# Rotary queries and keys projected as feature rows instead of token rows, and a list scheduler with other landing times

## The chip, the cores and the metric

The kernel runs on one core of one Trainium2 chip. The metric is device time in microseconds of that core. All arithmetic is float32; most large products are made of three passes over operands that were split into a high and a low part (type fp32r).

## What is computed

One layer of a hybrid encoder over 1024 tokens of width 1024: a SwiGLU network, a mixing part, a second SwiGLU network, each with an RMS norm before and behind it. The mixing part is what the change touches:

```python
z = _rmsnorm(h, mix_pre_g[l]) @ w_in[l]
y_att = _attention_group(z[..., :ATT_IN], cos, sin, attn_out_g[l])      # 8 heads of 64
y_rwkv = _rwkv7_group(z[..., ATT_IN:], ...)                             # 8 heads, two directions
mix = jnp.concatenate([y_att, y_rwkv], axis=-1) @ w_out[l]
...
def _rope(t, cos, sin):                      # queries and keys, per head
    half = t.shape[-1] // 2
    t1, t2 = t[..., :half], t[..., half:]
    return jnp.concatenate([t1 * c - t2 * s, t2 * c + t1 * s], axis=-1)
```

The first 1536 columns of `w_in` give queries, keys and values (512 each), the other 1920 feed the RWKV-7 scan. Attention is softmax over three dilated bands; the scan runs forward and backward in blocks.

## The kernel before, in words

The program is written as straight code, but nothing is issued while it runs. Each engine call is noted on a tape (`_Tape.note`); at the end `_Tape.order` chooses an order and `_Tape.play` issues it. So every instruction of the profile stands at one line, that of `play` (L512 before, L565 in the changed kernel), and instructions are told apart by their tiles.

The order comes from a list scheduler. `_Tape.cost` gives each operation a time on its engine (`took`), a time until others may use its result (`late`), and for transfers a time on the wire (`moved`). `_Tape.sweep` walks through time and gives each engine the ready operation of best rank; `_Tape.order` runs it forward and backward a few times, keeps the best order by its own reckoning, then adds the hand-set offsets of the table `LEADS` (from operation, to operation, offset of rank) and sweeps once more. On the chip each engine, and each queue of transfers, takes its own list strictly in turn; waits between engines follow from the data.

The stages in time: first network (to about 690 us of the span), projection of the scan's inputs (`project_rwkv`), projection of queries, keys and values (`project_tokens`), attention (`attention`, with `far` and `near`), the scan (`prep`, `solve`, `merge`, `chain`) interleaved with all of these from the projections on, the output projection (`project_attended`, `finish_unit`, `out_project`) and the second network.

In `project_tokens` a block of 256 columns of `w_in` is loaded (`columns`: tile `zraw`, split into `zh` and `zl`). For each of eight groups of 128 tokens, 24 matmuls of 256 columns make the bank `zq` with tokens as rows. For queries and keys ScalarE copies it to `zz`, VectorE multiplies it by two tables (`rope`, 32 loads) and adds (`zo`), TensorE turns it by two transposes (`zt`, with the identity), ScalarE copies the high part and a plain copy (`zts`), VectorE takes the low part, and GpSimd issues the stores: one to `d_qf` or `d_kf`, and two to `d_kk` for keys or four to `d_q` for queries, in rows of 128 floats. Values need only the copy and one store (`d_va`).

In `project_rwkv` the same kind of product is made the other way round: features are rows, two banks `zr` of 128 by 512 hold all 1024 tokens, and each of 48 matmuls is 512 columns wide.

Other names that the prediction speaks of: `X` (from `d_x`) is what a block's solve works on, by 62 small operations on `ttmp` and `Ti`, on GpSimd for blocks 1 to 5 and on VectorE for the others; its result goes to `d_t` and `d_tt` and comes back as `d` and `tt` for the matmuls `pa` and `pb`. `th_w`, `th_a`, `in` are loads of `prep`, `bk` and `pr` its products, `lp` and `bp` its matmuls, `lm` what is kept of `lp`. `xu`, `st` and `y` are the matmuls of the recurrence itself. `s`, `pt` and `po` (64 columns) are attention's scores, transposes and values. At its end `ya` goes to `d_ya`, comes back as `yat`, is scaled and turned (`yq`) and multiplied by the output weights (`wor`, split into `woh` and `wol`; `po` with 512 columns).

Of the kernel before, what the change touches and what calls it, by code (L numbers as in the profile page):

```python
# [32 lines left out]
def _ap(src, off, pat):  # L33
# [58 lines left out]
class _Op:  # L92
    __slots__ = ("eng", "method", "args", "kwargs", "out", "ins", "after", "preds", "succs", "took", "late", "load", "rank",
                 "left", "ready", "start", "end", "n", "moved", "follow", "taken", "frees", "grid", "cell", "port")


class _Tape:
# [3 lines left out]
    FREE, NEAR = ("ps_w",), 3000  # L101
    GATED = {"s3": 0, "s12": 0, "pt3": 0, "pt12": 0, "lp": 0, "bp": 0, "yq": 0, "gate": 1, "bonus": 1, "op": 2}

    def __init__(self, tc):
        self.tc, self.nc = tc, tc.nc
        self.ops, self.pools, self.home, self.stacks, self.now, self.hold = [], [], {}, {}, 0, []
        for name in self.NAMES:
            setattr(self, name, _Voice(self, name))
        self.masks = {}
        self.base, self.top = -(-tc.nc.sbuf_base // 32) * 32, tc.nc.sbuf_top  # L110
# [52 lines left out]
    def wire(self):  # L163
# [83 lines left out]
        for op in self.nodes:  # L247
            op.preds, op.succs = list(given[op]), []
# [5 lines left out]
    def cost(self, op):  # L254

        op.load = op.moved = 0
# [6 lines left out]
        if op.method == "dma_start":  # L263
# [7 lines left out]
            op.moved = max((9.5 * runs + 0.0366 * size) / 16, size / (3.6 * rows))  # L271
        elif op.eng == "tensor":
# [86 lines left out]
    def sweep(self, back=False):  # L359
# [11 lines left out]
        push, pop = heapq.heappush, heapq.heappop  # L371

# [17 lines left out]
        while True:  # L390
# [54 lines left out]
            if e == "tensor":  # L445
                took = self.pace(last, op, t - free[e])
                last, follow = op, op.follow
                if not back:
                    while t >= edge + 3413:
                        part = busy / 3413  # L450
                        cold, busy, edge = part < 0.56 or cold and part < 0.885, 0.0, edge + 3413
                    took = took * 2 if cold else took
                    busy += took * (0.5, 0.8, 1.0)[op.grid[0] // 64]
# [13 lines left out]
            settle(op, end)  # L467
            if not back:
# [12 lines left out]
    def order(self, rounds=5):  # L481
# [4 lines left out]
        for k in range(rounds):  # L486
            out, span = self.sweep()
            if best is None or span < best[1]:
                best = out, span, {op: (op.start, op.end) for op in out}, {op: op.rank for op in self.nodes}
# [6 lines left out]
        for op, (a, b) in best[2].items():  # L496
            op.start, op.end = a, b
# [9 lines left out]
    def play(self, ops):  # L507
# [3 lines left out]
        for op in ops:  # L511
            i = getattr(getattr(self.nc, op.eng), op.method)(*op.args, **op.kwargs).ins  # L512
# [144 lines left out]
class _Kernel:  # L657
# [264 lines left out]
    def columns(self, p, c0, n, tiles=None, tag="zraw", bufs=4):  # L922

        hl = tiles or [[p.tile([128, n], F32R, name="z" + c, tag="z" + c, bufs=12) for c in "hl"] for k in range(NK)]
# [26 lines left out]
    def project_tokens(self, p, psum, x):  # L951

        nc, V, A, G, T = self.nc, self.nc.vector, self.nc.scalar, self.nc.gpsimd, self.nc.tensor
        for b, g in [(b, g) for b in (1, 0, 2) for g in range(2)]:
            hl = self.columns(p, b * 512 + g * 256, 256)
            for t in range(NT):
                ts = slice(t * 128, t * 128 + 128)
                ps = psum.tile([128, 256], F32, name="zq", tag="w")
                self.token_major(ps, x, t, hl)
                z = p.tile([128, 4, 2, 32], F32, name="zz", tag="zz", bufs=3)  # L960
                A.activation(z.rearrange("p a b c -> p (a b c)"), ps, AF.Copy, scale=-HD ** -0.5 if b == 0 else 1.0)
                if b == 2:
                    G.dma_start(self.v_att[ts, g * 256:g * 256 + 256], z.rearrange("p a b c -> p (a b c)"))
                    continue
                cs = p.tile([128, 2, 2, 32], F32, name="rope", tag="rope", bufs=2)
                self.load(cs.rearrange("p a b c -> p (a b c)"), self.io["k_rope"][ts, :])
                o, y = (p.tile([128, 4, 2, 32], F32, name="z" + n, tag="z" + n, bufs=1) for n in "oy")
                V.tensor_tensor(o, z, cs[:, None, 0].to_broadcast([128, 4, 2, 32]), op=OP.mult)
                V.tensor_tensor(y, z[:, :, ::-1, :], cs[:, None, 1].to_broadcast([128, 4, 2, 32]), op=OP.mult)
                V.tensor_tensor(o, o, y, op=OP.add)  # L970
                q = psum.tile([128, 2, 128], F32, name="zt", tag="o")
                of = o.rearrange("p a b c -> p (a b c)")
                for i in range(2):
                    T.transpose(q[:, i, :], of[:, i * 128:(i + 1) * 128], self.ident)
                y = p.tile([128, 2, 128], F32, name="zts", tag="zts", bufs=2)
                w = p.tile([128, 2, 2, 128], F32R, name="zt", tag="zt", bufs=2)
                h, l = w[:, :, 0], w[:, :, 1]
                A.activation(h, q, AF.Copy)
                V.tensor_tensor(l, q, h, op=OP.subtract)
                A.activation(y, q, AF.Copy)  # L980
                G.dma_start((self.q_d, self.kt_d)[b][g * 2:g * 2 + 2, :, ts].rearrange("a p t -> p a t"), y)
                for d, v in zip(self.qk_d[b], (w, w[:, :, ::-1])):
                    for i in range(2):
                        G.dma_start(_ap(d, (g * 512 + i * 256) * S + t * 128, [[2 * S, 128], [S, 2], [1, 128]]),
                                    v[:, i].bitcast(F32))

    def project_rwkv(self, p, psum, x, blocks):

        nc, V, A, T = self.nc, self.nc.vector, self.nc.scalar, self.nc.tensor
        for c0, n in blocks:  # L990
            hl = self.columns(p, ATT + c0 * 128, n * 128)
            for ct in range(c0, c0 + n):
                cs = slice((ct - c0) * 128, (ct - c0 + 1) * 128)
                ps = [psum.tile([128, 512], F32, name="zr", tag="w") for half in range(2)]
                for k, (h, l) in enumerate(hl):
                    for half in range(2):
                        for i, (w, j) in enumerate(((h, 0), (h, 1), (l, 0))):
                            T.matmul(ps[half], w[:, cs], x[half][j][:, k, :], start=(k == 0 and i == 0),
                                     stop=(k == NK - 1 and i == 2))
# [907 lines left out]
```

## Time and profile before

| | |
|---|---|
| median of 3 runs | 2240.51 us (2238.98 to 2243.06) |
| the profiled execution | 2226.97 us, span 2225.2 us |
| mean granted TensorE clock | 0.985 |
| busy | TensorE 2138.5 us, weight loads 1776.4, VectorE 1551.0, ScalarE 1041.7, GpSimd 724.2 |

All times below are of the profiled execution, counted from the start of its span. A matmul's duration in the rows includes the way through the array, which overlaps the next one: what a matmul costs is the distance from one start to the next. A matmul of plain float32 stands as two records, so 32 records of `lp` are 16 calls. "q" behind an engine's name means its queue of transfers.

### The profile page before, as it was taken

The numbers are of one execution on the slowest core, as the hardware profiler recorded it, in microseconds if no ns is written. First come the engines' busy times: TensorE is split into PE (matmuls) and PEld (weight loads), VectorE is DVE, ScalarE is ACT, GpSimd is POOL, SyncE is SP. The second block draws the span as 40 slices with busy tenths as digits, with TensorE's granted clock in tenths as the row PEclk, the third lists the DMA queues.
The fourth block names the chain that finished last, engine by engine and source line by source line (L and its number), as shares of the span: only waits on it lengthen the run. The fifth ranks groups of instructions, "written<-read, shape, count | busy, mean of one in ns | idle before, by whom it ended". The sixth has DMA issues, their size and how long they took to land.

```text
span 2225.2 us, 41159 instructions
## 1 busy us (share of the span) xinstructions
PE 2138.5 (96%) x15236; PEld 1776.4 (80%) x15236; DVE 1551.0 (70%) x2630; ACT 1041.7 (47%) x2021; POOL 724.2 (33%) x1070
## 2 busy tenths in 40 slices
PE   7999999999999999999889998999899999999998
PEld 5888888888877887999777887777788888878886
DVE  8787778775575665764465567659987878877565
ACT  6333323354466655553556676456533233335453
POOL 2344444520000001569366571312053444441000
PEclk9999999999999999999899999999999999999999
DMA  5354454586563339875887656675454444558665
GB/s 151 127 181 152 154 168 142 185 276 201 174 206 105 131 149 279 229 231 164 232 223 199 180 154 169 168 258 167 123 180 142 169 158 142 171 171 288 195 206 171
DMA packets 370749, 404.52 MB, mean 182 GB/s; under 512 B 76402, under 2 KB 279026, under 8 KB 370548
## 3 DMA queue, kind: packets, MB, share of 16 engines
q1 hardware_dynamic: 320256, 294.79, 44.4%
q0 software_dynamic: 32240, 98.64, 12.4%
q10 hardware_dynamic: 18052, 8.46, 1.4%
q8 instruction: 120, 1.97, 0.4%
q14 instruction: 81, 0.66, 0.1%
HBM read 267.50 MB, written 134.28 MB: 181 GB/s over the span
## 4 chain that ended last, share of the span: by engine, by line
PE 73%; DVE 9%; DMA 6%; POOL 5%; issue 4%; ACT 3%; SPq 1%; ACTq 0%; DVEq 0%; POOLq 0%
PE gu L512 34%; PE pd L512 17%; PE zr L512 5%; PE po L512 3%; DVE row L512 3%; PE pt L512 2%; PE s L512 2%; PE lp L512 2%; POOL d_q L512 2%; PE xu L512 1%; DVE wl L512 1%; PE zq L512 1%; DVE s L512 1%; PE y L512 1%; POOL Ti L512 1%
## 5 line engine op out<-in xcount | busy, mean ns | idle before, releaser
L512 ACT ACTIVATE wh<-raw 128x512 fp32r<-128x512 f32 x264 | 161.5, 627 | 396.6 <-PE gu L512 257.7
L512 DVE TENSOR_TENSOR wl<-raw,wh 128x512 fp32r<-128x512 f32 x264 | 238.8, 917 | 73.7 <-PE gu L512 39.7
L512 DVE TENSOR_TENSOR row<-gu,row 128x512 f32<-128x512 f32 x308 | 203.1, 683 | 88.0 <-PE gu L512 50.7
L512 PE MATMUL gu<-xh,wl 128*128 128x512 f32 x704 | 239.3, 393 | 1.1 <-DVE wl L512 1.1
L512 POOL TENSOR_TENSOR row<-row 128x512 f32<-128x512 f32 x88 | 119.6, 1359 | 362.3 <-DVE row L512 324.0
L512 PE MATMUL gu<-xh,wh 128*128 128x512 f32 x704 | 234.5, 394 | 1.5 <-ACT xh L512 1.4
L512 PE MATMUL gu<-xl,wh 128*128 128x512 f32 x704 | 233.2, 392 | 1.7 <-DVE xl L512 1.7
L512 DVE TENSOR_TENSOR gwl<-graw,gwh 128x512 fp32r<-128x512 f32 (+1 forms) x176 | 114.0, 654 | 101.3 <-PE pd L512 84.1
L512 PE MATMUL pd<-gl,gwh 128*128 128x512 f32 x616 | 182.3, 392 | 0.0
L512 PE MATMUL pd<-gh,gwh 128*128 128x512 f32 x616 | 181.3, 391 | 0.4 <-ACT gh L512 0.4
L512 PE MATMUL pd<-gh,gwl 128*128 128x512 f32 x616 | 180.2, 391 | 0.7 <-DVE gwl L512 0.7
L512 ACT ACTIVATE gwh<-graw 128x512 fp32r<-128x512 f32 (+1 forms) x176 | 100.8, 575 | 146.6 <-PE pd L512 123.5
L512 PEld LDWEIGHTS gu<-xh,wl 128*128 128x128 f32 x704 | 132.8, 189 | 29.4 <-DVE wl L512 1.9
L512 PEld LDWEIGHTS gu<-xh,wh 128*128 128x128 f32 x704 | 132.5, 189 | 29.3 <-ACT xh L512 2.2
L512 PEld LDWEIGHTS gu<-xl,wh 128*128 128x128 f32 x704 | 132.5, 189 | 28.8 <-DVE xl L512 2.0
L512 POOL DMA_DIRECT2D d_hid<-row x154 | 84.8, 552 | 168.9 <-DVE row L512 166.0
L512 PEld LDWEIGHTS pd<-gh,gwl 128*128 128x128 f32 x616 | 116.1, 189 | 25.5 <-DVE gwl L512 1.1
L512 PEld LDWEIGHTS pd<-gl,gwh 128*128 128x128 f32 x616 | 116.0, 189 | 24.7 <-DVE gl L512 0.3
L512 PEld LDWEIGHTS pd<-gh,gwh 128*128 128x128 f32 x616 | 115.3, 188 | 24.8 <-ACT gh L512 0.8
L512 ACT ACTIVATE gh<-raw 128x512 fp32r<-128x512 f32 x160 | 99.5, 629 | 53.3 <-PE pd L512 31.8
L512 DVE TENSOR_TENSOR gl<-raw,gh 128x512 fp32r<-128x512 f32 x160 | 112.1, 711 | 15.3 <-ACT gh L512 15.1
L512 POOL TENSOR_TENSOR ws<-ws 128x512 f32<-128x512 f32 x88 | 121.5, 1381 | 2.8
(296 smaller groups left out, 5141.8 us busy)
## 6 DMA issues: line engine op xcount, KB each, us to landing
d_hid<-row POOLq DMA_DIRECT2D x154, 256.0 KB, 2.5
graw<-d_hid SPq DMA_DIRECT2D x132, 256.0 KB, 2.7
raw<-in_ffn_w_gate_dram SPq DMA_DIRECT2D x88, 256.0 KB, 3.1
raw<-in_ffn_w_up_dram SPq DMA_DIRECT2D x88, 256.0 KB, 3.2
ws<-in_ffn_w_down_dram SPq DMA_DIRECT2D x88, 256.0 KB, 3.7
d_ws<-ws POOLq DMA_DIRECT2D x88, 256.0 KB, 2.8
raw<-d_ws SPq DMA_DIRECT2D x88, 256.0 KB, 3.0
raw<-in_ffn_w_down_dram SPq DMA_DIRECT2D x66, 256.0 KB, 3.5
```

Of the source, the lines that this page charges most:

```text
L512: i = getattr(getattr(self.nc, op.eng), op.method)(*op.args, **op.kwargs).ins
```

## The change

`project_tokens` is left with the values. Queries and keys go to a new function, `project_heads`, ahead of it: `columns` as before, then `features` (the inner part of `project_rwkv`, made a function) gives for each pair of heads two banks with features as rows. The halves of a head lie 32 rows apart, so four copies of 32 rows each on ScalarE, scaled, put the other half's rows beside (`zy`); VectorE multiplies the bank by one table, GpSimd the copy by the other, VectorE adds (`zo`), ScalarE copies the high part and VectorE takes the low one (`zt`). The transposes and the copy `zts` are gone. The table is loaded once, 1 MB with features as rows. The stores are whole rows of 1024 floats on SyncE's queue: two for each pair of keys, three for each pair of queries.

The buffers `zraw` go from 4 to 3, `zh` and `zl` from 12 to 11; a 96-column tile that only took space is dropped.

In the scheduler a transfer's `late` depends on its kind and size and has 900 ns more (`SPARE`), and a load's wire time is stretched (`slow`). `LEADS` has 25 rows in place of 34, for the new numbering. The class `_Spare` and the code around it could put extra matmuls into gaps of TensorE; nothing makes one, so none is issued.

```diff
 LEADS = (
-    (165, 245, -11262), (278, 411, 5699), (301, 311, -2969), (425, 453, -5871), (4022, 4045, -7113),
...
+    (130, 157, 14327), (434, 485, -4800), (1581, 1591, 18529), (4285, 4286, -7275), (4305, 4317, -16401),
...
@@ cost
             op.moved = max((9.5 * runs + 0.0366 * size) / 16, size / (3.6 * rows))
+            if op.eng == "gpsimd":
+                op.late = 2150 - 0.9 * min(op.moved, 1000) + self.SPARE
+            elif x.tensor.name in self.home:
+                op.late, op.slow = 1700 + 0.46 * op.moved + self.SPARE, 1.28
+            else:
+                op.late = 900 + 1.05 * op.moved + self.SPARE
@@ sweep
             if op.moved and not back:
                 wire = max(wire, own) + op.moved
-                end = wire - op.moved
-                lanes[e == "gpsimd"].append(wire + op.late)
+                end = own + (wire - op.moved - own) * op.slow
+                lanes[e == "gpsimd"].append(end + op.moved + op.late)
...
+    def project_heads(self, p, psum, x):
+
+        nc, V, A, G = self.nc, self.nc.vector, self.nc.scalar, self.nc.gpsimd
+        turns = p.tile([128, 2, S], F32, name="rope", tag="rope", bufs=1)
+        self.load(turns, self.io["k_rope"].rearrange("(c p) t -> p c t", p=128))
+        for b, g in [(b, g) for b in (1, 0) for g in range(2)]:
             hl = self.columns(p, b * 512 + g * 256, 256)
...
+            for c in range(2):
+                ps = self.features(psum, x, hl, c)
+                o, y = p.tile([128, S], F32, name="zo", tag="us"), p.tile([128, S], F32, name="zy", tag="u", bufs=1)
+                w = p.tile([128, 2, S], F32R, name="zt", tag="zt", bufs=1)
+                for half in range(2):
+                    sl = slice(half * 512, half * 512 + 512)
+                    for q in range(0, 128, 32):
+                        A.activation(y[q:q + 32, sl], ps[half][q ^ 32:(q ^ 32) + 32], AF.Copy, scale=self.qk_scale[b])
+                    V.scalar_tensor_tensor(o[:, sl], ps[half], self.qk_scale[b], turns[:, 0, sl], op0=OP.mult, op1=OP.mult)
+                    G.tensor_tensor(y[:, sl], y[:, sl], turns[:, 1, sl], op=OP.mult)
+                    V.tensor_tensor(o[:, sl], o[:, sl], y[:, sl], op=OP.add)
+                    A.activation(w[:, 0, sl], o[:, sl], AF.Copy)
+                    V.tensor_tensor(w[:, 1, sl], o[:, sl], w[:, 0, sl], op=OP.subtract)
+                pr = g * 2 + c
+                nc.sync.dma_start((self.q_d, self.kt_d)[b][pr], o)
+                for d, v in zip(self.qk_d[b], (w, w[:, ::-1])):
+                    nc.sync.dma_start(_ap(d, pr * 256 * S, [[2 * S, 128], [S, 2], [1, S]]), v.bitcast(F32))
+
+    def features(self, psum, x, hl, c):
+
+        cs = slice(c * 128, (c + 1) * 128)
+        ps = [psum.tile([128, 512], F32, name="zr", tag="w") for half in range(2)]
+        for k, (h, l) in enumerate(hl):
+            for half in range(2):
+                for i, (w, j) in enumerate(((h, 0), (h, 1), (l, 0))):
+                    self.nc.tensor.matmul(ps[half], w[:, cs], x[half][j][:, k, :], start=(k == 0 and i == 0),
+                                          stop=(k == NK - 1 and i == 2))
+        return ps
@@ run
             self.project_rwkv(zr, po, x, [(4, 2), (6, 2), (0, 2), (2, 2), (8, 2), (10, 2)])
+            self.project_heads(zr, po, x)
             self.project_tokens(zr, po, x)
```

The order changes on every engine. Three places matter to the prediction. The first is GpSimd's list where the values are stored and the solve of block 1 ends. Before:

```order
L512 TENSOR_TENSOR Ti<-Ti,ttmp 128x16
L512 DMA d_t_169<-Ti 1024x1x16 x2
L512 DMA d_tt_181<-X 1024x1x32 x2
L512 DMA d_va<-zz 128x256
L512 DMA d_qf<-zts 128x2x128
L512 DMA d_va<-zz 128x256
L512 DMA d_q_130<-zt 256x1x128 x2
L512 DMA d_q_133<-zt 256x1x128
L512 DMA d_va<-zz 128x256
L512 DMA d_q_133<-zt 256x1x128
L512 DMA d_3018<-d_t_169 32x16x32 x2
L512 DMA tt_2369<-d_tt_181 32x16x32 x2
```

Now:

```order
L565 TENSOR_TENSOR Ti<-Ti,ttmp 128x16
L565 DMA d_t_169<-Ti 1024x1x16 x2
L565 DMA d_va<-zz 128x256 x2
L565 DMA d_tt_181<-X 1024x1x32 x2
L565 DMA d_2802<-d_t_169 32x16x32 x2
L565 DMA d_va<-zz 128x256 x2
L565 MEMSET Ti 128x512
L565 DMA tt_2154<-d_tt_181 32x16x32 x4
```

The stores of queries are gone from between the solve and the loads that `pa` waits for. Three of the sixteen `d_va` came after the load `d` before; six do now.

The second place is VectorE's list where the output weights are first split. Before (`in_3265` is the last block's second direction):

```order
L512 TENSOR_TENSOR lm<-lp,k_tri 128x512
L512 SCALAR_TENSOR_TENSOR wol<-wor,c_attn_out_g,woh 128x512 x2
L512 TENSOR_TENSOR Ti<-Ti,ttmp 128x13x10
L512 SCALAR_TENSOR_TENSOR th_a<-th_a,in_3265 128x512
L512 TENSOR_TENSOR ttmp<-X,Ti 128x120
L512 SCALAR_TENSOR_TENSOR bk<-th_a,th_w 128x8x64
```

Now (`in_3037` is the last block's first direction):

```order
L565 SCALAR_TENSOR_TENSOR bk<-bk,th_w 128x8x64
L565 TENSOR_SCALAR rs<-ss_a 128x64
L565 SCALAR_TENSOR_TENSOR th_a<-th_a,in_3037 128x512
L565 SCALAR_TENSOR_TENSOR bk<-th_a,th_w 128x8x64
L565 RECIPROCAL rs<-rs 128x64
L565 SCALAR_TENSOR_TENSOR wol<-wor,c_attn_out_g,woh 128x512
L565 TENSOR_TENSOR yat<-yat,rs 128x512
L565 SCALAR_TENSOR_TENSOR wol<-wor,c_attn_out_g,woh 128x512
L565 TENSOR_TENSOR sv<-st,gc 64x2x256 x2
```

The product `bk` that the next `lp` needs stood behind two `wol`; now it stands ahead of the first one, and the second direction's `bk` comes much later.

The third is TensorE's list between the end of attention and the first `yq`. Before:

```order
L512 MATMUL y<-lm,uv 64x64 x16
L512 MATMUL bp<-ident,bk 128x64 x3
L512 MATMUL lp<-pr,bk 128x128 x12
L512 MATMUL bp<-ident,bk 128x64 x5
L512 MATMUL y<-pr,sv 64x64 x16
L512 MATMUL lp<-pr,bk 128x128 x4
L512 MATMUL bp<-ident,bk 128x64 x8
L512 MATMUL st<-sv,ident 64x256 x4
L512 MATMUL lp<-pr,bk 128x128 x16
L512 MATMUL yq<-ident,yat 128x128 x4
```

Now:

```order
L565 MATMUL y<-pr,sv 64x64 x16
L565 MATMUL xu<-sv,lm 64x64 x8
L565 MATMUL lp<-pr,bk 128x128 x16
L565 MATMUL xu<-sv,lm 64x64 x8
L565 MATMUL pb<-tt_2154,d_3010 32x32 x32
L565 MATMUL bp<-ident,bk 128x64 x16
L565 MATMUL xu<-xs,tt_2154 64x64 x16
L565 MATMUL st<-uv,bt 64x64
L565 MATMUL y<-lm,uv 64x64 x16
L565 MATMUL st<-uv,bt 64x64 x15
L565 MATMUL yq<-ident,yat 128x128 x4
```

The last block's second `lp` has moved behind the first `yq`; in its place stand a merge (`pb`) and a step of the recurrence (`xu`, `st`, `y`).

More of the change, by code (lines that the diff above doesn't have):

```diff
@@ L93, with __init__ @@
     __slots__ = ("eng", "method", "args", "kwargs", "out", "ins", "after", "preds", "succs", "took", "late", "load", "rank",
-                 "left", "ready", "start", "end", "n", "moved", "follow", "taken", "frees", "grid", "cell", "port")
+                 "left", "ready", "start", "end", "n", "moved", "follow", "taken", "frees", "grid", "cell", "port", "opens", "shuts", "idle",
+                 "slow")
+class _Spare:
+    def __init__(self, tape, out, w, x):
+        self.name, self.call = out.tensor.name, lambda: tape.nc.tensor.matmul(out, w, x, start=True, stop=True)
+        tape.spares.append(self)
 class _Tape:
@@ L101 @@
     FREE, NEAR = ("ps_w",), 3000
+    GAP, TURN, SPARE = 400, 120, 900
     GATED = {"s3": 0, "s12": 0, "pt3": 0, "pt12": 0, "lp": 0, "bp": 0, "yq": 0, "gate": 1, "bonus": 1, "op": 2}
@@ L254, in cost @@
     def cost(self, op):
-        op.load = op.moved = 0
+        op.load, op.moved, op.slow = 0, 0, 1.0
         op.grid, op.cell, op.port = None, None, False
@@ L371, in sweep @@
         push, pop = heapq.heappush, heapq.heappop
+        spare = [[r.wait, 0.0] for r in self.spares]
         def settle(op, end):
@@ L448, in sweep @@
                 if not back:
-                    while t >= edge + 3413:
-                        part = busy / 3413
-                        cold, busy, edge = part < 0.56 or cold and part < 0.885, 0.0, edge + 3413
+                    op.idle, u = None, free[e]
+                    while True:
+                        turn = None
+                        if t - u >= self.GAP or op.idle and t - u >= 2 * self.TURN + 150:
+                            turn = next((i for i, r in enumerate(spare) if r[0] == 0 and r[1] <= u), None)
+                        at = t if turn is None else u
+                        while at >= edge + 3413:
+                            part = busy / 3413
+                            cold, busy, edge = part < 0.56 or cold and part < 0.885, 0.0, edge + 3413
+                        if turn is None:
+                            break
+                        op.idle = (op.idle or []) + [turn]
+                        busy, u = busy + self.TURN * (1 + cold), u + self.TURN * (1 + cold)
                     took = took * 2 if cold else took
@@ L467, in sweep @@
             settle(op, end)
+            for i, r in enumerate(spare):
+                if not back and op.opens >> i & 1:
+                    r[0], r[1] = r[0] - 1, max(r[1], end + op.late)
+                if op.shuts >> i & 1:
+                    r[0] = -1
             if not back:
@@ L488, in order @@
             if best is None or span < best[1]:
-                best = out, span, {op: (op.start, op.end) for op in out}, {op: op.rank for op in self.nodes}
+                best = out, span, {op: (op.start, op.end, op.idle) for op in out}, {op: op.rank for op in self.nodes}
             if k + 1 < rounds:
@@ L495, in order @@
                     op.rank = op.end if op.eng else op.ready
-        for op, (a, b) in best[2].items():
-            op.start, op.end = a, b
+        for op, (a, b, c) in best[2].items():
+            op.start, op.end, op.idle = a, b, c
         for op, rank in best[3].items():
@@ L511, in play @@
         for op in ops:
+            for r in op.idle or ():
+                i = self.spares[r].call().ins
+                if op.eng in last:
+                    self.tc.add_manual_dep(i, last[op.eng].name, info, reason="order")
+                last[op.eng] = i
             i = getattr(getattr(self.nc, op.eng), op.method)(*op.args, **op.kwargs).ins
@@ L992, in project_rwkv @@
             for ct in range(c0, c0 + n):
[L993 to L999, printed above, removed]
+                ps = self.features(psum, x, hl, ct - c0)
                 u = p.tile([128, S], F32, name="u", tag="u", bufs=1)
```

67 lines of the change are left out of this document (30 added, 37 removed), and 11 rows, old and new, of the table LEADS.

## The prediction

> **What bounds the kernel now.** I read the page's busy times first, then the stages, then each stretch in which TensorE stood still.
>
> ```profile
> span 2225.2 us, 41159 instructions
> PE 2138.5 (96%) x15236; PEld 1776.4 (80%) x15236; DVE 1551.0 (70%) x2630; ACT 1041.7 (47%) x2021; POOL 724.2 (33%) x1070
> PE 73%; DVE 9%; DMA 6%; POOL 5%; issue 4%; ACT 3%; SPq 1%; ACTq 0%; DVEq 0%; POOLq 0%
> 890.00:1075.00 185.00, 177.45 (x1791) 171.53 (x1789) 102.98 (x264) 79.89 (x205) 136.48 (x230) 0.98 0.69 201
> 1605.00:1990.00 385.00, 379.62 (x1667) 312.71 (x1666) 307.45 (x405) 120.89 (x203) 166.34 (x191) 1.00 0.47 158
> ```
>
> TensorE is busy for 96% of the span and is 73% of the chain that ended last. The last two rows are stages (columns after the length: busy TensorE, weight loads, VectorE, ScalarE, GpSimd, granted clock, share of transfers). The second network loses 5 us in 385; the changed projection, 890 to 1075, loses 7.5 in 185. So TensorE work taken out of that stage should come off the time, and the 87 us in which TensorE idles are all that a better order can win. The dearest of these are at two places:
>
> ```profile
> 1074.28 0.22 PE L512 MATMUL pa<-d,lm 32*32 32x32 f32 x2 [2.60 <-ACT th_a L512]
> 1075.96 0.47 PE L512 MATMUL pa<-d,lm 32*32 32x32 f32 x9 [1.46 <-DMA d<-d_t]
> 1387.64 2.68 PE L512 MATMUL lp<-pr,bk 64*128 64x128 f32 x11 [7.73 <-DVE bk L512]
> 1075.00:1090.00 15.00, 11.96 (x231) 11.34 (x233) 2.76 (x7) 8.38 (x14) 1.66 (x5) 0.54 0.95 306
> 1375.00:1388.00 13.00, 5.27 (x76) 4.49 (x73) 11.79 (x30) 6.08 (x12) 2.25 (x2) 0.78 0.63 181
> 1388.00:1396.00 8.00, 8.00 (x43) 7.32 (x42) 7.77 (x22) 4.67 (x7) 0.00 (x0) 0.50 0.50 126
> 1396.00:1405.00 9.00, 8.66 (x38) 6.65 (x38) 6.10 (x19) 3.15 (x6) 2.36 (x3) 0.81 0.88 233
> ```
>
> The bracket is the idle time before the row and its releaser. A gap costs twice: after the 7.73 us the granted clock is 0.50 for 8 us and 0.81 for 9 more.
>
> **The matmuls of queries and keys.** Starts in dense runs give the price of one:
>
> ```profile
> 892.45 3.72 PE zq L512 x31
> 784.20 16.61 PE zr L512 x73
> 963.01 0.28 PE L512 MATMUL zq<-zh,xl 128*128 128x256 f32 x1
> 963.13 0.38 PE L512 MATMUL zt<-ident,zo 128*128 128x128 f32 x2
> 963.26 0.36 PE L512 MATMUL zq<-zh,xh 128*128 128x256 f32 x1
> 963.47 0.28 PE L512 MATMUL zq<-zl,xh 128*128 128x256 f32 x1
> L512 PE MATMUL zq<-zh,xh 128*128 128x256 f32 x384 | 96.2, 290 | 1.2 <-ACT zz L512 1.2
> L512 PE MATMUL zt<-ident,zo 128*128 128x128 f32 x64 | 13.2, 278 | 0.6 <-DVE ttmp L512 0.6
> ```
>
> 3.72/31 is 0.120 us for 256 columns, 16.61/73 is 0.2275 for 512. Of the 3 x 384 `zq` two thirds, 768, are queries and keys: 92.2 us. A pair of transposes stretches two steps of 0.12 (963.01 to 963.26 to 963.47, 0.46 in all) by 0.22: 32 pairs, 7.0 us. In their place stand 384 matmuls of 512 columns, the `zr` form, which is in the trace: 87.4 us. Sum: 87.4 - 99.2 = -11.8 us. In a stage where TensorE is busy 177 of 185 us this is time on the path.
>
> **The work beside them** goes into the same stage:
>
> ```profile
> L512 ACT ACTIVATE zz<-zq 128x256 f32<-128x256 f32 x48 | 17.6, 384 | 43.8 <-PE zq L512 39.2 <-issue 2.5 <-ACT zts L512 0.9
> L512 ACT ACTIVATE zts<-zt 128x256 f32<-128x256 f32 x32 | 12.2, 381 | 6.9 <-DMA d_qf<-zts 4.7 <-PE zt L512 1.4 <-ACT zz L512 0.5
> L512 ACT COPY d<-pa 32x512 f32<-32x512 f32 x16 | 9.9, 616 | 3.9 <-PE pa L512 3.6
> L512 ACT ACTIVATE gh<-raw 128x512 fp32r<-128x512 f32 x160 | 99.5, 629 | 53.3 <-PE pd L512 31.8 <-DMA raw<-in_ffn_w_down_dram 20.2 <-DVE gl L512 0.8
> L512 DVE TENSOR_TENSOR zo<-zo,zy 128x256 f32<-128x256 f32 x32 | 14.1, 440 | 0.4
> L512 DVE SCALAR_TENSOR_TENSOR xl<-pt,c_mix_pre_g,xh 128x512 fp32r<-128x512 f32 x16 | 11.3, 744 | 4.9 <-ACT xh L512 4.8
> L512 DVE TENSOR_TENSOR gl<-raw,gh 128x512 fp32r<-128x512 f32 x160 | 112.1, 711 | 15.3 <-ACT gh L512 15.1
> L512 POOL TENSOR_TENSOR row<-row 128x512 f32<-128x512 f32 x88 | 119.6, 1359 | 362.3 <-DVE row L512 324.0 <-ACT wh L512 35.6 <-PE gu L512 1.9
> L512 POOL DMA_DIRECT2D d_q<-zt x64 | 55.8, 1065 | 0.5 <-DVE zo L512 0.4
> L512 POOL DMA_DIRECT2D d_kk<-zt x32 | 22.8, 769 | 4.5 <-DVE ttmp L512 2.7 <-DVE Ti L512 1.4 <-DVE zt L512 0.4
> L512 POOL DMA_DIRECT2D d_qf<-zts x16 | 15.9, 1001 | 9.1 <-ACT zts L512 8.3 <-ACT zh L512 0.8
> L512 POOL DMA_DIRECT2D d_kf<-zts x16 | 12.3, 771 | 25.1 <-ACT zts L512 20.3 <-ACT zz L512 4.2 <-issue 0.4
> ```
>
> ScalarE loses 96 copies of about 0.383, 36.8 us, and gains 64 copies of 32 rows (nearest row: `d<-pa`, 0.616) and 16 high parts (0.629): 39.4 + 10.1 = 49.5, so 12.7 us more on an engine that is busy 80 of 185. VectorE loses four operations of about 0.44 for each of 32 groups, 56 us, and gains 16 times 0.744 + 2 x 0.711, 35 us. GpSimd loses 106.8 us of issuing and gains 16 x 1.359 = 21.7. SyncE's queue gets 20 stores and loses 31 table loads. On the path I take all of it at 0: a pair of heads now keeps TensorE for 48 x 0.2275 = 10.9 us, and needs 6.2 us of ScalarE and about 4.4 of VectorE. If that cover is gone, the rival below has the price.
>
> **The table load.** The 1 MB table now stands in SyncE's list behind the first three pieces of weights of the stage, where transfers had been idle and TensorE already waits:
>
> ```profile
> 690.00:715.00 25.00, 24.56 (x118) 20.16 (x118) 5.52 (x9) 8.62 (x15) 0.00 (x0) 1.00 0.00 1
> 720.71 1.22 PE L512 MATMUL zr<-xh,zh 128*128 128x512 f32 x2 [4.41 <-ACT zh L512]
> ```
>
> At the 306 GB/s of the row at 1075 it takes 3.4 us, by which pieces four to eight land later; three pieces are 18 matmuls, 4.1 us of work. Bounds 0 and +3.4; I take +1.5, since part lies behind that work.
>
> **The first place, 1074 to 1090.**
>
> ```profile
> 1000.00:1040.00 40.00, 38.76 (x322) 38.27 (x321) 21.52 (x46) 13.85 (x40) 39.74 (x73) 1.00 0.59 186
> ```
>
> GpSimd, the fifth busy time, has no free moment in the 40 us before. `pa` waits for the solve's way through memory, which GpSimd's issues of query stores delay: the solve's last rows have `d_q`, `d_qf` and `d_va` between them, and the load `d` comes after thirteen of sixteen `d_va`. Now no query store is left there and `d` comes after ten, six times 24 x 0.120 = 17 us of value matmuls from the end. All that can be won is 2.60 + 1.46 us of gaps and 12 x (1 - 0.54) = 5.5 of clock, 9.6; nothing, if `th_a`, or the loads of values behind `d_va`, are the next to be late. I take -5.
>
> **The second place, 1375 to 1405.** VectorE's `bk` stood behind two `wol`, and these behind a load that SyncE could only issue when the load of `yat` ahead of it had its data:
>
> ```profile
> 1376.61 4.10 DMA d_ya<-ya
> 1380.76 2.93 DMA wor<-in_w_out_dram
> ```
>
> Now `bk` is ahead of the first `wol`. The most to win is 7.73 + 8.0 x 0.5 + 8.66 x 0.19 = 13.4 us. But what is next late is known: `yq` needs the last head's way to memory and back (4.10 and then a load), and the recurrence's `xu` stands in TensorE's list behind it, ahead of the other matmuls. The list between holds about as much work as before. I take less than half, -6.
>
> **Everything else that the other order moves** has no row before: 0, with 15 us either way, about what one stall like the second costs. Sum: -11.8 + 1.5 - 5 - 6 = -21.3. The profiled execution took 2226.97 us, 1.8 more than its span, and would become 2205.7. The median of the runs is 13.5 above it, so for the median I forecast 2240.5 - 21.3 = **2219 us**. A difference under 0.2%, 4.5 us, can't be told from no change here.
>
> **The rivals.**
>
> *The stalls only move* (chance 0.22): the TensorE work goes, the two places lose as much at `yq` and at the values' loads, and the table costs its 1.5: 2240.5 - 10.3 = 2230. For it: in the row at 1075 transfers are busy 0.95 at 306 GB/s, and the values still come last.
>
> *The banks come free late* (0.13, the slower side). In `project_heads` a pair's two banks are free only after eight copies of 0.616, 4.9 us, and the two products on VectorE; only four such banks are there, and `lp`, `bp`, `pa` and `pb` take from the same. If each of the eight pairs makes TensorE wait 2 to 3 us, that is 16 to 24 us, and it decides as soon as it exceeds 1.3 us per pair: 2240.5 - 10.3 + 20 = about 2250 with the two places unmended. Against it: ScalarE has 4.7 us to spare per pair, and `project_rwkv` runs the same product on the same four banks with 5.7 us lost in 175.
>
> ```profile
> 715.00:890.00 175.00, 169.32 (x924) 137.47 (x923) 107.07 (x166) 102.91 (x195) 12.34 (x25) 0.99 0.56 182
> L512 DVE TENSOR_TENSOR wl<-raw,wh 128x512 fp32r<-128x512 f32 x264 | 238.8, 917 | 73.7 <-PE gu L512 39.7 <-ACT wh L512 32.5 <-issue 1.1
> ```
>
> A second hand on it: the same VectorE form takes 0.917 (`wl`) where GpSimd computes and 0.711 (`gl`, above) where it hardly does, so GpSimd's 16 new products can slow VectorE's 32 new two-input operations; at 0.2 each that is 0.8 us per pair, within the spare time. The Trainium skill ("SBUF — State Buffer", section "SBUF: two separate sides") says that a VectorE operation with two SBUF inputs and a GpSimd operation that reads SBUF exclude each other for a whole instruction. The two rows agree in direction. By that rule in full, 2 x 1.359 = 2.7 us per pair, VectorE would need 7.1 of 10.9 us, still no wait on TensorE by itself, which is why this rival has no more than its 0.13.
>
> *The gain is eaten in SyncE's queue* (0.10, no change, 2240): a 1 MB store that waits for VectorE holds the loads of `prep` behind it, and the recurrence comes late by some 10 us. For it: a 768 KB transfer takes 5.5 us to land.
>
> ```profile
> in<-d_rk SPq DMA_DIRECT2D x16, 768.0 KB, 5.5
> ```
>
> Against it: 31 loads leave SyncE's queue at the same time, and each of the 20 stores has its own pair's 10.9 us of matmuls to wait under.
>
> *The new landing times mend more than the two places* (0.05): 2197, with both in full and some 10 us of other waits for transfers.
>
> That the scheduler's part does nothing is excluded: the orders differ at all three places.
>
> **How the numbers follow.** The forecast's own case has 0.50 and 2206 to 2228. Faster by over 0.2%: 0.50 + 0.22 + 0.05 = 0.77; within: 0.10; slower: 0.13. The range for 8 in 10 goes from 2198 (both places in full, nothing new) to 2243 (the gain eaten).
>
> **What would show it.** `zr` 960 matmuls and `zv` 384 in place of 1152 `zq`, dense runs at 0.2275 us, no `zt` on TensorE; GpSimd under 60 us busy in the projection stage; no wait of `lp` for `bk` over 2 us near the end of attention, and a granted clock above 0.9 there; `pa` right behind the last `zv` without a wait for `d`. I am wrong if TensorE waits for ScalarE's copies between the pairs, or if a gap of over 5 us stands at a place that had none.

## The result and the profile after

The changed kernel takes 2208.0 us (median of 2207.16 to 2215.44) where the kernel before took 2239.7: ratio 0.987, 95% interval 0.984 to 0.990. A second comparison gave 0.987 (0.984 to 0.990). The forecast was 2219, range 2198 to 2243. From profiled execution to profiled execution it is 2226.97 to 2207.16, -19.8 us, where the sum had -21.3.

Of the page of the changed kernel (span 2205.4 us):

```profile
PE 2130.4 (97%) x14788; PEld 1751.8 (79%) x14788; DVE 1490.4 (68%) x2550; ACT 1058.5 (48%) x2007; POOL 662.3 (30%) x958
```

The stages, cut at the first `zr`, the last matmul of the projection, the first `yq`, the last `xu` and the end. Columns: length, busy time of TensorE, weight loads, VectorE, ScalarE, GpSimd, clock, transfers, GB/s. Before:

```profile
0.00:720.70 720.70, 696.06 (x3096) 568.95 (x3096) 523.11 (x758) 310.48 (x545) 201.46 (x239) 1.00 0.53 171
720.70:1070.60 349.90, 344.18 (x2688) 307.30 (x2688) 205.72 (x426) 173.85 (x381) 144.42 (x248) 0.99 0.63 193
1070.60:1394.00 323.40, 292.83 (x5027) 246.04 (x5025) 205.90 (x515) 210.33 (x477) 155.24 (x336) 0.94 0.72 196
1394.00:1484.30 90.30, 88.46 (x1117) 68.89 (x1118) 52.58 (x134) 47.29 (x88) 24.25 (x28) 0.97 0.69 203
1484.30:2225.00 740.70, 716.98 (x3320) 585.20 (x3316) 563.69 (x800) 299.70 (x533) 198.80 (x221) 0.99 0.55 178
```

After:

```profile
0.00:714.30 714.30, 693.67 (x3096) 568.88 (x3096) 504.48 (x758) 312.12 (x545) 199.59 (x239) 1.00 0.54 173
714.30:1055.10 340.80, 335.69 (x2271) 280.22 (x2272) 191.99 (x346) 188.57 (x365) 82.63 (x144) 0.99 0.61 196
1055.10:1356.30 301.20, 278.14 (x4707) 235.19 (x4705) 174.33 (x443) 201.36 (x460) 152.69 (x326) 0.92 0.72 196
1356.30:1467.40 111.10, 105.42 (x1401) 81.48 (x1400) 75.78 (x200) 55.09 (x100) 23.88 (x28) 0.99 0.62 176
1467.40:2205.00 737.60, 717.51 (x3324) 586.03 (x3318) 543.83 (x805) 301.38 (x541) 203.53 (x223) 0.99 0.55 182
```

The first network, of which no operation is changed, is 6.4 us shorter. The projections are 9.1 shorter. Attention and the scan together (third and fourth row) take 412.3 us for 413.7: work was moved behind the first `yq`, and of the two places' 11 us almost nothing is seen. The rest gives 3.1.

Waits of TensorE in the changed kernel (the time in brackets is the idle time before the row):

```profile
714.31 1.22 PE L565 MATMUL zr<-xh,zh 128*128 128x512 f32 x2 [4.41 <-ACT zh L565]
1008.35 0.39 PE L565 MATMUL zv<-zh,xh 128*128 128x256 f32 x1 [1.10 <-ACT zy L565]
1060.07 0.22 PE L565 MATMUL pb<-tt,d 32*32 32x32 f32 x2 [2.89 <-issue]
1109.30 0.66 PE L565 MATMUL pt<-ident,sb 128*128 128x128 f32 x4 [2.15 <-ACT sb L565]
1131.50 1.76 PE L565 MATMUL po<-vn,e 128*64 128x64 f32 x28 [5.90 <-DVE ya L565]
1142.38 0.97 PE L565 MATMUL pt<-ident,sb 128*128 128x128 f32 x5 [3.76 <-ACT sb L565]
1352.05 0.48 PE L565 MATMUL st<-uv,bt 128*64 128x64 f32 x2 [3.07 <-ACT uv L565]
```

The 7.73 us before `lp` are gone, and `pa` no longer waits for `d`. In their place stand four other waits, one of 5.90 us where there was none. Behind the 2.89 us of `pb` the granted clock is 0.54 from 1060 to 1075, as it was from 1075 to 1090 before.

### The profile page after: what moved, and what is told of

It reads as the page before. It is cut to its first block, busy times and chain, and to the rows that moved or that the text cites. A ratio compares the mean times of both kernels' runs of the same rounds, so it can differ in the third digit from the quotient of the medians.

```text
span 2205.4 us, 39830 instructions
## 1 busy us (share of the span) xinstructions
PE 2130.4 (97%) x14788; PEld 1751.8 (79%) x14788; DVE 1490.4 (68%) x2550; ACT 1058.5 (48%) x2007; POOL 662.3 (30%) x958
## 5 line engine op out<-in xcount | busy, mean ns | idle before, releaser
L565 PE MATMUL gu<-xh,wh 128*128 128x512 f32 x704 | 251.5, 393 | 0.2 <-DVE row L565 0.2
L565 PE MATMUL gu<-xl,wh 128*128 128x512 f32 x704 | 251.6, 392 | 0.0
L565 PE MATMUL gu<-xh,wl 128*128 128x512 f32 x704 | 249.0, 391 | 0.1
L565 DVE TENSOR_TENSOR wl<-raw,wh 128x512 fp32r<-128x512 f32 x264 | 208.6, 810 | 9.3 <-ACT wh L565 6.8
L565 PE MATMUL pd<-gl,gwh 128*128 128x512 f32 x616 | 189.3, 391 | 0.0
L565 PE MATMUL pd<-gh,gwh 128*128 128x512 f32 x616 | 188.4, 390 | 0.4 <-ACT gh L565 0.4
L565 PE MATMUL pd<-gh,gwl 128*128 128x512 f32 x616 | 187.4, 390 | 0.0
L565 DVE TENSOR_TENSOR gl<-raw,gh 128x512 fp32r<-128x512 f32 x160 | 110.8, 704 | 18.8 <-ACT gh L565 18.3
L565 PE MATMUL zr<-xh,zh 128*128 128x512 f32 x320 | 105.6, 401 | 5.9 <-ACT zh L565 4.4
```

## The experiments

The steps of the prediction have letters here: A, the matmuls of queries and keys; B, the work beside them; C, the table load; D and E, the first and the second place; F, everything else that the order moves. A ratio is to the kernel before, and in brackets stands its 95% interval.

### The kernel before once more

> The kernel before, unchanged, profiled a second time. Its first profiled execution (2226.97 us) lay 13.5 us under the median of its runs, while the changed kernel's (2207.16 us) lies at its median, so the two profiles differ by 19.8 us and the medians by 31.7. Theory: the missing 12 us are stalls that vary between executions at the two places the prediction names, where late transfers decide (the wait of pa for d near 1075, of lp for bk near 1388). A profile at about 2240 then shows these two gaps longer by some 12 us together, and all other landmarks within 1 us. Rival: the difference is spread over the kernel (clock, many waits); then the two gaps are as before (2.60 + 1.46 and 7.73 us) and every stage is some tenths of a per cent longer. If this profile too comes at 2227, it tells nothing about this. Ratio of the times 1.000.

Measured: ratio 0.999 (0.997 to 1.001); the kernel's own runs on this chip spread from 2222.6 to 2242.7 us. The profiled one took 2234.04, 7.1 more than the first. Two stretches, of the first profile and then of this one, with the two named waits of this one:

```profile
1070.00:1100.00 30.00, 22.50 (x396) 20.61 (x394) 14.54 (x27) 17.82 (x36) 6.66 (x13) 0.77 0.94 286
1160.00:1300.00 140.00, 130.06 (x2252) 107.61 (x2252) 87.62 (x210) 92.50 (x216) 91.08 (x196) 0.98 0.73 194
```

```profile
1070.00:1100.00 30.00, 24.12 (x347) 22.06 (x346) 11.22 (x21) 15.74 (x31) 8.92 (x16) 0.66 0.96 281
1160.00:1300.00 140.00, 129.43 (x2122) 107.13 (x2119) 85.58 (x204) 86.40 (x203) 85.58 (x185) 0.93 0.70 186
1077.16 0.22 PE L512 MATMUL pa<-d,lm 32*32 32x32 f32 x2 [3.16 <-DMA d<-d_t]
1395.15 6.48 PE L512 MATMUL lp<-pr,bk 64*128 64x128 f32 x32 [8.18 <-DVE bk L512]
```

The two named gaps are as long as before (3.16 + 1.28 and 8.18 us). From the first `zr` to the last `xu` idle time is 1 us shorter, but the busy time lost to a lower clock (busy x (1 - clock), summed over windows of 4 us) is 28.2 us for 20.5. The theory is wrong: these two executions differ by the clock, not by the waits. The difference between medians can therefore hold some us of clock that a pair of single profiles does not show.

### The second place, VectorE alone

```diff
 VectorE:
+th_a<-th_a,in
+bk<-th_a,th_w
 wol<-wor,c_attn_out_g,woh x2
-th_a<-th_a,in
-bk<-th_a,th_w
```

> The kernel before with one move: VectorE's th_a and bk of that place stand ahead of the two wol, all else in the old order. It measures step E alone (the second place, max -13.4 us, taken as -6). The prediction's step: -6, between -3 and -13, with the wait of lp for bk gone and the granted clock from 1388 to 1405 near 1. Rival, the stalls only move: the gap of 7.73 us is gone, but yq or the recurrence behind it waits as long, and the last xu still comes at about 1484 us of the span: 0, within 2 us.

Measured: ratio 1.000 (0.998 to 1.002), and the wait did not even go. VectorE, TensorE and ScalarE there:

```profile
1385.40 0.69 DVE L512 SCALAR_TENSOR_TENSOR th_a<-th_a,in 128x512 f32<-128x512 f32 x1 [2.71 <-ACT th_a L512]
1386.96 6.48 PE L512 MATMUL lp<-pr,bk 64*128 64x128 f32 x32 [7.56 <-DVE bk L512]
1383.21 0.72 ACT L512 ACTIVATE woh<-wor,c_attn_out_g 128x512 fp32r<-128x512 f32 x1 [1.62 <-DMA wor<-in_w_out_dram]
1384.89 0.48 ACT L512 ACTIVATE th_a<-th_a,ka,kah 128x128 f32<-128x128 f32 x1
```

`th_a` on VectorE needs four pieces from ScalarE, and the fourth stood in ScalarE's list behind two `woh`, which wait for the same late `wor`. I had read the list of one engine only.

### The second place, both engines

```diff
 ScalarE:
 th_a<-th_a,ka,kah x3
+th_a<-th_a,ka,kah
+bk<-bk
 woh<-wor,c_attn_out_g x2
-th_a<-th_a,ka,kah
-bk<-bk
```

with VectorE's move as in the run before.

> The kernel before with the second place untied on both engines. The run that moved only VectorE's th_a and bk ahead of the two wol still waited 7.56 us there: VectorE's th_a now waited for ScalarE, whose last th_a and copy of bk stand behind two woh, and these behind the same late load wor. So here ScalarE's last th_a and its bk stand ahead of the two woh as well, all else as before. This prices step E of the prediction (-6, at most -13.4). Theory one, the step: -4 to -13 us, the wait of lp for bk under 2 us. Theory two, the stalls only move: that wait is gone or shorter, but yq and the matmuls of the output weights behind it wait as long for the same load, the last xu comes as late: 0, within 2 us.

Measured: ratio 1.001 (0.999 to 1.002). The wait falls by 3 us, and what stands behind it takes them:

```profile
1395.43 6.48 PE L512 MATMUL lp<-pr,bk 64*128 64x128 f32 x32 [4.75 <-DVE bk L512]
1402.99 1.09 PE L512 MATMUL yq<-ident,yat 128*128 128x128 f32 x4 [1.08 <-issue]
1406.17 1.22 PE L512 MATMUL po<-woh,yah 128*128 128x512 f32 x2 [1.27 <-DVE Ti L512]
1396.00:1404.00 8.00, 6.92 (x35) 6.33 (x34) 7.38 (x22) 3.59 (x5) 0.00 (x0) 0.50 0.55 157
```

The clock is 0.50 for the 8 us after it as before. VectorE's `th_a` now starts 0.6 us after ScalarE's last piece and `bk` right behind it: what is left is the chain itself, from `bp` and `pr` through `bk` and `th_a` to `bk` on three engines, with other operations of the scan between them on VectorE (busy 8.97 of the 9 us from 1386), and TensorE's list holds nothing ahead of `lp` to fill it. Theory two holds: this place is worth 0, within 5 us, to a move in these two lists. What it would be worth to have the wait gone is not shown, since 4.75 us of it stayed.

### The first network in the new order

The order of 5090 operations of the first network, on all engines, was taken from the changed kernel; everything behind them stands as before.

> The kernel before with only the first network in the changed kernel's order, on all engines; projection, attention, scan and second network keep their order and their code. In the two traces the first zr came at 720.7 us before and at 714.3 us after, though not one operation of the first network differs: the prediction had this at 0 (step F). Theory: these 6.4 us are the order's alone and carry through to the end: -6.4 us, between -4 and -8 (ratio 0.997), the four waits of gu for VectorE's row of 0.82 us gone. Rival: the scan and the transfers behind the first network have their own due times, so that the earlier start is lost by the last xu: 0, within 2 us.

Measured: 2223.7 us against 2233.3, ratio 0.996 (0.994 to 0.998). The waits of 0.82 us are gone, as is one of 2.37, and the first `zr` comes 5.6 us earlier. Before, and then in this run:

```profile
151.82 0.47 PE L512 MATMUL gu<-t6h,wh 128*128 128x512 f32 x1 [0.82 <-DVE row L512]
```

```profile
715.11 1.22 PE L512 MATMUL zr<-xh,zh 128*128 128x512 f32 x2 [4.41 <-ACT zh L512]
```

Idle time ahead of it is only 2.2 us shorter (22.4 for 24.6), since other waits came, one of 4.13 us. The earlier start does carry through to the end, as the theory says; the interval reaches from 4 to 15 us, so the 9.6 measured can't be told from the 6.4 expected.

### The 32-row copies doubled

```diff
+            if op.eng == "scalar" and op.out[0].tensor.name.rsplit("_", 1)[0] == "zy":
+                i = self.nc.scalar.activation(*op.args, **op.kwargs).ins
+                self.tc.add_manual_dep(i, last["scalar"].name, info, reason="order")
+                last["scalar"] = i
```

> The changed kernel with each of the 64 copies of 32 rows (zy) on ScalarE done twice, which doubles what the prediction hid beside the matmuls (step B at 0): 8 x 0.59 = 4.7 us more of ScalarE for each pair of heads, 37.8 us in all. Theory (the copies lie beside 10.9 us of matmuls per pair): of a pair's 10.9 us ScalarE needs 4.7 + 1.3 us for copies and high parts and some 1.5 for the weights' halves, 7.5 of 10.9; with 12.2 it is short by 1.3 us per pair, so the kernel loses about 10 us (5 to 16). Rival (the banks come free late already): the wait is on the path now, and all 37.8 us come on top, 30 to 40 us.

Measured: 2249.5 us, ratio 1.006 (1.004 to 1.009) to the kernel before: by the ratios 43 us more than the changed kernel. The projections alone take 388.7 us for 340.8:

```profile
713.10:1101.80 388.70, 356.58 (x2274) 295.20 (x2274) 190.47 (x346) 225.58 (x429) 82.66 (x144) 0.93 0.53 172
1046.33 0.58 PE L565 MATMUL zv<-zh,xh 128*128 128x256 f32 x1 [7.34 <-ACT zy L570]
1028.79 0.33 SPq L565 DMA_DIRECT2D d_qf<-zo  x1
1030.18 0.94 SPq L565 DMA_DIRECT2D d_q<-zt  x2
1031.22 9.39 SPq L565 DMA_DIRECT2D zraw<-in_w_in_dram  x6
1038.27 1.16 ACT L565 ACTIVATE zh<-zraw 128x256 fp32r<-128x256 f32 x3 [7.93 <-DMA zraw<-in_w_in_dram]
```

The size is the rival's and a little more, but the mechanism is not the rival's: in the changed kernel TensorE waits for a `zy` only some 2.5 us in all. The copies are one link of a ring. Late copies make `zo` late, SyncE's stores of `zo` and `zt` hold the next `zraw` loads behind them, ScalarE waits 7.93 us for those with the next copies behind in its list, and the granted clock of the stage is 0.93 for 0.99. By sums of busy time there was 4.7 us to spare per pair; by the order of the lists there was next to none. The change also took away one of four `zraw` buffers; what that adds to the ring was not tried.

### Projection and landing times, crossed

Four kernels: old or new projection, old or new landing times in the scheduler (its code as a whole from the one kernel or the other), each without its table of offsets.

```diff
 LEADS = (
-    (165, 245, -11262), (278, 411, 5699), (301, 311, -2969), (425, 453, -5871), (4022, 4045, -7113),
...
+)
```

> The kernel before without its table of hand-set offsets: old projection, old landing times in the scheduler. First of four that cross the two parts of the change (projection; landing times), all without offsets, since each table fits one numbering only. It is the base of the other three, and by itself it says what the offsets were worth: by the prediction's view of single stalls of 5 to 13 us that an order can mend, 10 to 60 us slower than the kernel before.

> Old projection, new landing times in the scheduler, no offsets. Prediction (rank of the parts: matmuls -11.8 certain, order -11 with 15 us either way): against the old times without offsets some -10 us, the waits for transfers fewer. Rival: landing times that are 0.9 us later and scattered only shuffle the order, and without the offsets search behind it the result is within 5 us or worse.

> New projection, old landing times, no offsets. Against the old projection with old landing times, by step A: -9 to -12 us for the matmuls of queries and keys, which do not depend on the order, if nothing else moves. In the trace the stage from the first zr to the last value matmul should be some 9 us shorter than in the kernel with the old projection and the same scheduler, whatever the total is. Rival: with another order the copies of 32 rows or the stores come late and the stage is as long as before.

> New projection, new landing times, no offsets: the changed kernel without its hand-set table. Theory: the two parts add, so new_new - old_new = new_old - old_old = -9 to -12 us. Rival: the new landing times pay only with the new projection, whose stores left GpSimd's queue; then new_new gains more over new_old than old_new over old_old. What is left to the changed kernel (2208 us) is the worth of its offsets.

Measured on one chip, the kernel before at 2233.4 us:

| | old landing times | new landing times |
|---|---|---|
| old projection | 2236.1; 1.001 (0.999 to 1.003) | 2206.7; 0.988 (0.985 to 0.991) |
| new projection | 2244.3; 1.004 (1.002 to 1.007) | 2211.1; 0.990 (0.987 to 0.994) |

The landing times bring 29.4 us with the old projection and 33.2 with the new. The projection costs 8.1 us with the old times. With the new ones it is 4.4 slower, which the intervals can't tell from 0, but no run of the new projection (2207.2 to 2214.3) is 11.8 below one of the old (2204.7 to 2208.8). The offsets were worth 2.7 us before and, by the ratios, 7 in the changed kernel (0.987 for 0.990), both within the intervals; so I was wrong on them too. By the intervals, the old projection with new times is as fast as the whole change.

Each of the four kernels is a single order of all its operations, so part of every difference can be the chance of that order; the landing times gain about as much with either projection. The gain with the old projection lies in waits and clock: over the whole span TensorE idles 72.0 us for 91.8, and the clock's loss, summed as above, is 20.1 for 36.1.

The stage of the projections, from the first `zr` to its last matmul, in the order old/old, new projection with old times, old projection with new times, new/new:

```profile
718.20:1067.98 349.78, 344.67 (x2689) 306.90 (x2690) 205.39 (x427) 174.95 (x383) 146.03 (x249) 0.99 0.63 193
717.10:1075.81 358.71, 344.57 (x2274) 286.13 (x2276) 198.90 (x347) 191.23 (x368) 86.27 (x144) 0.97 0.59 187
715.30:1060.28 344.98, 343.03 (x2689) 306.65 (x2690) 198.70 (x425) 171.08 (x381) 137.24 (x232) 0.99 0.63 194
716.20:1057.24 341.04, 336.60 (x2274) 280.83 (x2276) 191.83 (x346) 188.73 (x365) 83.11 (x144) 0.99 0.61 196
```

The expected 9 us less in this stage did not come. With the old times the new projection makes it 8.9 us longer, as the rival had it: TensorE idles 14.1 us for 5.1, and 5.7 of them it waits for a `zy`. With the new times the stage is 3.9 us shorter.

Where the matmuls went, from the first `zr` to the last `xu`, old projection with new times and then new with new:

```profile
715.30:1464.30 749.00, 722.66 (x8823) 618.48 (x8823) 451.28 (x1069) 426.22 (x937) 329.62 (x609) 0.98 0.68 196
1353.75 0.45 PE L558 MATMUL yq<-ident,yat 128*128 128x128 f32 x1 [5.99 <-DVE yat L558]
```

```profile
716.20:1465.00 748.80, 719.12 (x8375) 597.10 (x8375) 439.95 (x986) 443.10 (x921) 256.98 (x496) 0.97 0.66 194
```

With the old projection, too, `lp` no longer waits for `bk`; `yq` waits 5.99 us a little later. Idle time is length less busy, 26.3 and 29.7 us. The clock's loss, summed as above, is 15.0 and 21.4. What remains is work at full clock: 707.7 and 697.7. The other matmuls of the two stretches are the same. So 10 us of work did leave, and 3.4 us of waits and 6.4 of clock came for them. (With the old times the same sum gives -5.6 of work, +13.5 of waits and +5.6 of clock; its split is good to some us only.)

### The new stalls untied

On VectorE the ten operations from `M` to `ya` go ahead of the scan's `bk`, `bk`, `th_a`, `bk`; on ScalarE and GpSimd:

```diff
 ScalarE:
+c<-c x2
 th_a<-th_a,ka,kah x4
 bk<-bk
-c<-c x2
 GpSimd:
 ya<-ya,far
+far<-ya
 ttmp<-X,Ti
-far<-ya
```

> The changed kernel unchanged, on the same chip as the next two, to compare them with: ratio to the kernel before 0.987 as first measured (0.984 to 0.990).

> The changed kernel with its two largest new stalls untied by three moves in the lists: on VectorE the ten operations of attention from M to ya ahead of the scan's bk, bk, th_a and bk; on ScalarE the two c ahead of the four th_a; on GpSimd the product far, for which ss_a and behind it attention's sb wait on VectorE, ahead of a ttmp that waits for a late transfer. In the changed kernel po waits 5.90 us for ya at 1131.50, pt 3.76 us for sb at 1142.38, and the clock is 0.74 and 0.91 in the 40 us from 1120. Theory (the gain of the matmuls went into these stalls and comes back when they are gone): 3.9 + 3.8 us of waits and up to 7 of clock, -6 to -13 us against the changed kernel. Rival (the stalls only move): the scan's bk, now 3 us later, or the next banks make TensorE wait as long: within 3 us of the changed kernel.

Measured: 2205.7 us against 2203.6 for the changed kernel beside it, ratios 0.987 (0.985 to 0.990) and 0.987 (0.984 to 0.990). Changed kernel, and with the moves:

```profile
1137.88 1.76 PE L565 MATMUL po<-vn,e 128*64 128x64 f32 x28 [5.66 <-DVE ya L565]
1137.00:1160.00 23.00, 21.66 (x291) 17.90 (x292) 12.58 (x40) 11.92 (x31) 18.60 (x48) 0.89 0.69 185
```

```profile
1135.27 1.76 PE L565 MATMUL po<-vn,e 128*64 128x64 f32 x28 [3.30 <-DVE ya L565]
1137.00:1160.00 23.00, 21.75 (x244) 17.56 (x242) 12.86 (x37) 12.26 (x32) 17.81 (x47) 0.76 0.56 149
```

The wait is 2.4 us shorter and `po` comes 2.6 earlier, but a lower clock takes it back in the next 23 us. The second wait, 3.76 in the first profile, was gone in the unchanged kernel's second one too. The stalls only move.

> The kernel of the run before (attention's ya first), and half of the 32-row copies (zy) put from ScalarE on VectorE, at the same places of the order: ScalarE loses 32 x 0.59 = 18.9 us in the projection stage, VectorE gains about as much (it is busy for 192 of 341 us there). Doubling the copies cost 41 us, so they are not covered. Theory (the banks of the pairs come free late, on ScalarE): the waits of the stage for zy and bt, 4.1 us, go: -2 to -6 us against the run before. Rival (ScalarE is only just early enough, and VectorE's own chain is now as long): 0 to +5 us.

The edit turns every second of the four copies into VectorE's `tensor_scalar`. Measured: 2213.3 us, ratio 0.991 (0.988 to 0.994), 7.6 above the run without it. In the profile the projection's last matmul ends 7 us later (1062.8 for 1055.6): the rival, and a little more. Sharing the copies does not speed up the stage; VectorE's own place in the ring is as tight. But this profiled execution, the fastest of the six with 2205.0 us, has the last `xu` 1.2 us earlier than the run without the edit, so it does not show where the 7.6 us of the medians lie.

## Why the prediction was right, and where it was not

The time was right, its composition was not. Step by step:

| step | forecast | what the runs showed |
|---|---|---|
| A, matmuls | -11.8 | 10 us of work left; the time did not: +4.4 and +8.1 in the crossed runs |
| B, work beside them | 0 | no cover to spare: 38 us more of copies cost 43 |
| C, table | +1.5 | 0: the first `zr` waits 4.41 us before and after, and no later one waits for a piece of weights |
| D, first place | -5 | `pa`'s 2.60 + 1.46 us are gone, `pb` waits 2.89 and the clock behind it is 0.54 as before; not tried alone |
| E, second place | -6 | 0 for moves on one and on two engines, which left 7.56 and 4.75 us of the wait; its full removal was not tried alone |
| F, everything else | 0, 15 either way | about -29 from the landing times; the new order of the first network alone gave -9.6 (-4 to -15) |

**Step A** failed at the words "this is time on the path". Durations were right (`zr` 960, `zv` 384, 0.2275 us in dense runs), and from the kernel before to the changed one the stage became 9.1 us shorter. But in the crossed runs it was 3.9 us shorter with the new landing times and 8.9 longer with the old ones, so not even the length of the stage follows from its matmuls. And it is followed by 400 us in which attention and scan run in chains through four engines and memory. There the new projection with new times took 3.8 us more than the old one (407.8 for 404.0, the clock's loss 18.3 for 12.7), and with the copies shared a projection that ended 7 us later still had its last `xu` 1.2 us earlier. Whether TensorE waits there because it is ahead, or because the order behind the stage is another one, no run tells apart.

**Step B** was put at 0 by comparing sums per pair of heads. Order inside the lists was the thing to read: which copy stands behind which load, which load behind which store. Of the signs, `lp` no longer waits for `bk`, the granted clock near the end of attention is 0.91 (1340 to 1380), and `pa` runs right behind the last `zv`, as forecast. The sentence that I would be wrong if a gap over 5 us stood where none was came true at 1131.50; TensorE's waits for the copies came true in small, 2.5 us in all; and GpSimd was busy 70.6 us from 890 to 1055, not under 60.

The profile also bears on a rule that the prediction weighed. In the changed kernel:

```profile
L565 DVE TENSOR_TENSOR zt<-zo,zt 128x512 fp32r<-128x512 f32 x16 | 12.8, 800 | 7.0 <-ACT zt L565 6.8
L565 DVE TENSOR_TENSOR zo<-zo,zy 128x512 f32<-128x512 f32 x16 | 11.8, 738 | 10.9 <-POOL zy L565 10.9
```

These two-input operations took 0.80 and 0.74 us on the mean, where 0.711 had been assumed. Three of the 32 ran while GpSimd had one of its products and took 1.22 to 1.23 us; five ran beside small operations of the solve and took 0.85 to 0.93; the others took 0.68 to 0.69. The Trainium skill's rule of whole-instruction exclusion ("SBUF — State Buffer", section "SBUF: two separate sides") would give far more if every one met a GpSimd product; three do.

**Steps D and E** took gaps that one profile showed as a price. E had also the wrong cause, the wait of one engine where two stood behind the same load. **Step F** held the gain. Its bound of 15 us, "about what one stall like the second costs", was too small for costs that reorder all 18,000 operations. The rival whose mechanism came nearest is the one with the least chance, *the new landing times mend more than the two places*; but of the 19 us between the profile of the kernel before and that of the old projection with new times, 5.4 lie in the first network and 5.2 in the projections. *The stalls only move* comes nearest to what is seen at both places, and *the banks come free late* showed as the price of the next microsecond, not of this one.

Between the two profiles alone the composition looks right as well: 11.7 us less idle time (span less busy, 75.0 for 86.7), 9.7 less work at full clock and 1.6 more lost to the clock. Only the crossed runs show that an order gains as much without the work removed. So that the sum fell so near is an accident of signs: 23 us credited to A, D and E, of which the crossed runs and the moves show none at the end, and some 29 not credited to F. The medians lie 28 to 32 us apart, so even the sum is short by 6 to 10. The lower end of the range, 2198, does not follow from its words either: both places in full and nothing new is -11.8 + 1.5 - 9.6 - 13.4 = -33.3, which gives 2207.

Not settled: which of the landing times does it, and how much of the gain is the chance of the orders that came out. Whether the new orders also spread less is not shown: the old projection with new times ran from 2204.7 to 2208.8 us in four runs, but the new projection with old times from 2242.6 to 2248.3 in eight, while the kernel before, with many more runs, had 2222.6 to 2253.2.

## What to carry to other kernels

Work taken from the busiest engine comes off the time only if what follows can start earlier: cross the edit with the order before crediting it, since an order made with better costs gave 29 us here and the removed matmuls none. A gap in one profile is not its price; shortening two of them by 2.4 and 3 us moved the time by nothing measurable. When an operation waits, follow each of its inputs back through the list of the engine that makes it, not only the list in which it stands.

## What the runs showed of the hardware

The granted clock was halved here without any idle time. In the second profile of the changed kernel TensorE is busy through these windows, and so it is in old projection with new times (last row):

```profile
1206.46 2.02 PE L565 MATMUL s<-kp,qp 64*64 64x64 f32 x32
1208.41 1.20 PE L565 MATMUL pa<-d,lm 32*32 32x32 f32 x64
1212.86 1.92 PE L565 MATMUL pb<-tt,d 32*32 32x32 f32 x64
1208.00:1224.00 16.00, 16.00 (x230) 13.88 (x228) 6.77 (x16) 7.71 (x14) 0.00 (x0) 0.57 0.46 113
```

```profile
1208.00:1224.00 16.00, 16.00 (x378) 13.61 (x380) 7.50 (x24) 11.82 (x26) 1.04 (x1) 1.00 0.99 248
```

The first had matmuls of 32 and 64 rows and columns standing close together ahead of it. Some 7 us were lost there with nothing for a list of gaps to show; that small matmuls are the cause was not tried alone. The Trainium skill ("TensorE: Matmul & The Clock Gate", section "What's actually happening") has the half rate follow an idle window of about 3.4 us; this trace does not agree, since no idle time stands in the 16 us or in the 8 before them.

What follows one and the same wait differs. The one of `pt` at 1109 was 2.15 us in the first profile of the changed kernel, with clock 0.94 over the 20 us from 1108, and 1.84 us in the second, with 0.58:

```profile
1108.00:1128.00 20.00, 15.02 (x190) 12.29 (x190) 12.20 (x30) 13.86 (x33) 15.85 (x39) 0.94 0.95 264
```

```profile
1108.00:1128.00 20.00, 17.94 (x136) 14.81 (x136) 8.54 (x19) 8.22 (x20) 16.65 (x43) 0.58 0.98 274
```

Busy 17.94 us at 0.58 is 7.5 us of loss, behind a shorter wait.
